# Four gate tiles of a decoder's last embedding as seven block products

## The chip, the cores and the metric

The kernel is one launch on one core of a Trainium2 chip. The core has TensorE (PE in the profile; PEld is its weight load), VectorE (DVE), ScalarE (ACT), GpSimd (POOL) and SyncE (SP, which issues the DMAs here). The metric is device time in microseconds (us): the median of several executions. A profiled execution gives one trace, whose span runs from the first to the last instruction.

## The reference

One inference step of a decoder with two layers, in float32, for 512 prompt rows and 32 sample rows, 1024 wide. Each layer ends with a gated embedding; the last one is the last thing that is computed:

```python
for i in range(DEPTH):
    h = h + 0.5 * swiglu(rmsnorm(h, ffn1_norm[i]), ffn1_w1[i], ffn1_w3[i], ffn1_w2[i])
    ...                                   # gMLP in layer 0, attention in layer 1
    h = h + 0.5 * swiglu(rmsnorm(h, ffn2_norm[i]), ffn2_w1[i], ffn2_w3[i], ffn2_w2[i])
    gate = jax.nn.sigmoid(rmsnorm(h, ple_norm[i]) @ ple_w_gate[i])     # 1024 x 1024
    h = h + gate * (pe[i] @ ple_w_proj[i])                             # 256 x 1024
```

## The kernel before

**Tiling.** The residual stream h is held transposed: 8 tiles of 128 features by 544 columns (512 prompt and 32 sample rows; T = 544, HT = 272), two tiles to a buffer. A float32 product is made of three: each operand is split into a rounded high part and the rest, and hi x hi, hi x lo and lo x hi are added in PSUM. Each is done in two halves of 272 columns, so a product over 1024 features takes 8 x 3 x 2 = 48 matmuls per output tile, and one over 256 features 12 (`mm`, L273: hi x hi at L286, hi x lo at L290, lo x hi at L292).

**Weights** come as a stream of units. `_load` (L206) issues a unit's DMA from SyncE; `_sum` (L219, VectorE at L228) adds or subtracts two raw blocks where a unit is a sum; `_split` (L231) rounds it on ScalarE (L242) and takes the rest on VectorE (L243), for a unit of 1024 columns in one instruction each. `prepare` (L247) does so some units ahead of the unit that TensorE takes, as the three numbers in `self.ahead` say: splits, sums, loads.

**Norm.** The normalised input is never formed. `prep` (L338) multiplies h with the gain and splits it, as soon as a tile of h is final; the root mean square enters at the end, as a factor on each column. `tile_rstd` (L395) slips four matmuls with ones (L408) into the first tile's product, and the reciprocal root is made by ScalarE (L386, with a load of its function table) and VectorE (L389 to L393).

**Seven block products.** The feed-forward layers compute 2 x 2 blocks of an output (two features' blocks by two column halves) with seven block products instead of eight, in the Winograd form. `seven` (L193) describes the weight units ("1", "2", "4" are raw blocks, "5", "6", "7", "3" are sums), `forms` (L347) makes the operands on the other side for two tiles of h at a time (two L352 on ScalarE; L356, L358, L359 on VectorE; two splits, L330 and L331), and the order of the products is `SEVEN = "1562734"`. One block product has 4 x 3 x 2 = 24 matmuls. Some results accumulate in one PSUM buffer: "6" goes on top of "1" once that has been copied out, and so on; the copies and additions are L547 to L561 there.

**The last embedding** is `ple` (L745) with layer 1. For c = 0 to 6 it computes a gate tile over 8 feature tiles (48 matmuls), multiplies it with the norm's factor (L766, VectorE) and takes the sigmoid (L767, ScalarE). From c = 2 on, the product of the embedding input with its projection for tile c - 2 follows (12 matmuls), is multiplied with the gate (L777), added to h (L778) and written out (L1474). Behind c = 6 come the products of tiles 5 and 6, and `ple_last` (L728) does tile 7 in column halves, so that the end of the first half overlaps the second: 48 and 12 matmuls at L723, VectorE at L736, L741 and L742, two writes at L743.

**Order.** Each engine executes its instructions strictly in the order in which they are queued. In the feed-forward layers that order is written by hand. In the embedding a scheduler of the compiler sets it, from its own times; the program then holds it fixed. Buffers come from pools: 45 large ones (big), 8 of one tile (tmp), 3 of PSUM in two banks (ps), 2 of one bank (pb); an instruction that needs a buffer waits until its last reader is through.

Of the kernel before, what the change touches and what calls it, by code (L numbers as in the profile page):

```python
# [138 lines left out]
class Builder:  # L139
# [207 lines left out]
    def forms(self, h, gcol, n, xs):  # L347
# [3 lines left out]
        for a in range(2):  # L351
# [12 lines left out]
                "5": half(f13, 0), "7": half(f13, 1), "6": half(f24, 0), "4": half(f24, 1)}  # L364
    def ssq(self, acc, h, cols=slice(0, T), first=False):
# [362 lines left out]
    def ple_last(self, h, gates, rstd, xs, wp, pp, y):  # L728

        nc, tt = self.nc, self.nc.vector.tensor_tensor  # L730
        c = NC_ - 1
        a = self.tmp()
        outs = [self.pb(), self.pb()]
        self.cols_mm(outs, self.blocks(self.unit()), xs)
        for (u, v), out in zip(COLS, outs):
# [4 lines left out]
        for (u, v), out in zip(COLS, outs):  # L740
            tt(halves(a[:, u:v]), unwoven(out[:, :v - u]), halves(a[:, u:v]), ALU.mult)  # L741
            tt(h[c][:, u:v], h[c][:, u:v], a[:, u:v], ALU.add)  # L742
            nc.sync.dma_start(out=y[c][:, u:v], in_=h[c][:, u:v])  # L743

    def ple(self, h, box, layer, on_chunk):  # L745
        nc = self.nc
        xs = self.pairs(box)
        pp = []
        for c in range(2):
            raw = self.tmp()  # L750
            nc.sync.dma_start(out=raw, in_=self.i["pe"][layer, c])
            pair = self.big(F32R)
            self.split_pair(pair, raw)
            pp.append((pair[:, 0, :], pair[:, 1, :]))
        rstd, gates, wp = None, [], []
        last = layer == 1
        for c in range(NC_ + 2):
# [15 lines left out]
            for n in (range(c - 2, c + 1) if last and c == NC_ - 2 else [c - 2] if c >= 2 else ()):  # L773
# [597 lines left out]
    def build(self):  # L1371
# [7 lines left out]
        def ple_units(n):  # L1379
            for c in range(NC_):  # L1380
# [93 lines left out]
        self.ple(h, box, 1, lambda c: nc.sync.dma_start(out=o["y"][c], in_=h[c]))  # L1474
# [123 lines left out]
```

## Time and profile before

| | us |
|---|---|
| median of 3 runs | 1932.85 |
| lowest and highest of them | 1932.0, 1933.58 |
| the profiled execution | 1931.65 |
| its span | 1929.9 |
| TensorE busy in it | 1905.2 |
| VectorE, ScalarE, GpSimd busy | 1478.6, 949.0, 143.4 |

A group of instructions reads: line, engine, operation, output<-input, partitions x elements and type, number | busy us in total, mean ns of one | idle time of the engine just before them, and what ended most of it. A row of the time line reads: start, us from the first start to the last end, engine, line, operation, number, and in brackets how long the engine had been idle and what released it. A row of a table by stage gives the stage, its length, busy us of each engine with the number of its instructions, the granted share of TensorE's clock, and the DMA engines' share and rate. Line numbers are those of the kernel before.

### The profile page before, as it was taken

How to read it: one execution, taken by the hardware profiler on the slowest of the kernel's cores; microseconds unless marked ns; L12 is line 12 of the kernel's file. 1: busy time of each engine (PE TensorE's matmuls, PEld its weight loads, DVE VectorE, ACT ScalarE, POOL GpSimd, SP SyncE). 2: the span in 40 equal slices, each digit the busy share in tenths (PEclk: the TensorE clock that was granted, in tenths of full speed). 3: DMA queues.
4: the chain of work that ended last, by engine and by line, in shares of the span. 5: the costliest groups of instructions: out<-in, count | busy, mean ns of one | idle time of the engine just before them, and what ended most of it. 6: DMA issues, size and time to landing. Idle time of an engine off the chain costs nothing.

```text
span 1929.9 us, 38975 instructions
## 1 busy us (share of the span) xinstructions
PE 1905.2 (99%) x16508; PEld 1869.9 (97%) x16508; DVE 1478.6 (77%) x1863; ACT 949.0 (49%) x1428; POOL 143.4 (7%) x190
## 2 busy tenths in 40 slices
PE   9999999999999999999999999999999999999999
PEld 8999999999999999999999999999977899999999
DVE  7878888556788888866578888887476888788874
ACT  7545444424555344454466444444374754444561
POOL 0000000400100000023000000002131300000020
PEclk9999999999999999999999999999999999999999
DMA  5233234312223232531484332323769332323431
GB/s 196 78 120 110 89 120 157 97 48 88 88 99 119 79 111 89 162 112 39 150 306 141 121 110 99 121 83 126 229 211 328 101 110 78 121 94 105 133 109 47
DMA packets 95743, 237.61 MB, mean 123 GB/s; under 512 B 11874, under 2 KB 29570, under 8 KB 95570
## 3 DMA queue, kind: packets, MB, share of 16 engines
q1 hardware_dynamic: 95426, 235.08, 36.6%
q8 instruction: 130, 2.13, 0.4%
q14 instruction: 43, 0.35, 0.1%
q10 hardware_dynamic: 144, 0.04, 0.0%
HBM read 218.65 MB, written 16.44 MB: 122 GB/s over the span
## 4 chain that ended last, share of the span: by engine, by line
PE 88%; DVE 6%; ACT 3%; issue 2%; DMA 1%; SPq 1%; POOL 0%; DVEq 0%; ACTq 0%; POOLq 0%
PE ps L539 31%; PE ps L286 15%; PE ps L292 15%; PE ps L290 15%; PE pb L539 5%; DVE big L243 2%; ACT big L242 1%; DVE big L228 1%; PE ps L892 1%; PE ps L893 1%; PE ps L894 1%; DVE big L331 1%; DVE big L497 0%; DMA tmp<-rows 0%; PE ps L1286 0%
## 5 line engine op out<-in xcount | busy, mean ns | idle before, releaser
L539 PE MATMUL ps<-big,big 128*128 128x272 f32 x5616 | 674.1, 279 | 5.9 <-DVE big L556 3.5
L539 PEld LDWEIGHTS ps<-big,big 128*128 128x128 f32 x5616 | 660.8, 189 | 7.0 <-issue 4.0
L243 DVE TENSOR_TENSOR big<-big,big 128x1024 fp32r<-128x1024 f32 (+2 forms) x537 | 587.1, 1096 | 91.0 <-ACT big L242 89.3
L242 ACT CAST big<-big 128x1024 fp32r<-128x1024 f32 (+2 forms) x537 | 484.2, 928 | 270.2 <-DVE big L228 267.7
L286 PE MATMUL ps<-big,big 128*128 128x272 f32 x2668 | 530.2, 280 | 2.9 <-ACT big L242 2.5
L292 PE MATMUL ps<-big,big 128*128 128x272 f32 x2668 | 528.3, 279 | 2.5 <-DVE big L243 2.3
L290 PE MATMUL ps<-big,big 128*128 128x272 f32 x2668 | 527.3, 279 | 0.3 <-DVE big L343 0.3
L286 PEld LDWEIGHTS ps<-big,big 128*128 128x128 f32 x2668 | 407.1, 189 | 7.8 <-ACT big L242 4.4
L292 PEld LDWEIGHTS ps<-big,big 128*128 128x128 f32 x2668 | 406.9, 189 | 4.5 <-DVE big L243 4.1
L290 PEld LDWEIGHTS ps<-big,big 128*128 128x128 f32 x2668 | 406.9, 189 | 0.7 <-DVE big L343 0.7
L371 POOL TENSOR_TENSOR st<-st,tmp 128x544 f32<-128x544 f32 (+1 forms) x63 | 87.4, 1387 | 1477.0 <-ACT tmp L369 1476.7
L228 DVE TENSOR_TENSOR big<-big,big 128x1024 f32<-128x1024 f32 x156 | 190.1, 1219 | 0.0
L578 DVE SCALAR_TENSOR_TENSOR big<-ps,big 128x544 f32<-128x544 f32 x160 | 115.3, 721 | 75.8 <-PE ps L292 75.8
L500 ACT ACTIVATE big<-big 128x544 f32<-128x544 f32 x88 | 57.9, 659 | 145.8 <-DVE big L497 144.6
L497 DVE TENSOR_TENSOR big<-big,st 128x1088 f32<-128x1088 f32 x88 | 113.6, 1293 | 3.9 <-ACT big L561 2.0
L547 ACT COPY tmp<-ps 128x544 f32<-128x544 f32 x117 | 71.5, 611 | 89.7 <-PE ps L539 89.7
L539 PE MATMUL pb<-big,big 128*128 128x272 f32 x936 | 114.8, 279 | 0.0
L539 PEld LDWEIGHTS pb<-big,big 128*128 128x128 f32 x936 | 111.3, 189 | 0.0
L342 ACT ACTIVATE big<-big,gains 128x544 fp32r<-128x544 f32 (+1 forms) x80 | 55.5, 702 | 91.3 <-DVE big L578 55.2
L331 DVE TENSOR_TENSOR big<-big,big 128x544 fp32r<-128x544 f32 (+1 forms) x112 | 79.2, 713 | 21.7 <-ACT big L330 21.5
L343 DVE SCALAR_TENSOR_TENSOR big<-big,gains,big 128x544 fp32r<-128x544 f32 (+1 forms) x80 | 64.6, 816 | 24.2 <-ACT big L342 24.2
L330 ACT CAST big<-big 128x544 fp32r<-128x544 f32 (+1 forms) x112 | 71.2, 643 | 18.9 <-DVE big L503 14.9
(218 smaller groups left out, 1388.5 us busy)
## 6 DMA issues: line engine op xcount, KB each, us to landing
big<-in_w SPq DMA_DIRECT2D x156, 512.0 KB
big<-in_w2a SPq DMA_DIRECT2D x64, 512.0 KB
big<-in_w2b SPq DMA_DIRECT2D x32, 384.0 KB
big<-in_w13p SPq DMA_DIRECT2D x16, 512.0 KB
big<-in_win SPq DMA_DIRECT2D x16, 512.0 KB
big<-in_wg SPq DMA_DIRECT2D x16, 512.0 KB
big<-in_ck SPq DMA_DIRECT2D x16, 512.0 KB
big<-in_cv SPq DMA_DIRECT2D x16, 512.0 KB
```

Of the source, the lines that this page charges most:

```text
L228: self.nc.vector.tensor_tensor(t, a, b, ALU.add if op == "+" else ALU.subtract)
L242: self.nc.scalar.copy(hi, src)
L243: self.nc.vector.tensor_tensor(lo, src, hi.bitcast(F32), ALU.subtract)
L286: i = nc.tensor.matmul(o, wh, xh[:, b], start=s, stop=False)
L290: nc.tensor.matmul(o, wh, xl[:, b], start=False, stop=False)
L292: nc.tensor.matmul(o, wl, xh[:, b], start=False, stop=e)
L331: self.nc.vector.tensor_tensor(pair[:, 1, cols], src, pair[:, 0, cols].bitcast(F32), ALU.subtract)
L371: nc.gpsimd.tensor_tensor(acc[:, cols], acc[:, cols], sq, ALU.add)
L497: tt(g, g, rstd.unsqueeze(1).broadcast_to([P, 2, T]), ALU.mult)
L539: nc.tensor.matmul(turns(dst[w]), a[:, c], woven(b), start=k in "152" and kp == 0 and n == 0, stop=kp == NKP - 1 and n == 2, skip_group_ch ...
L547: nc.scalar.copy(t["r" + k], t["C" if k == "5" else "A"])
L578: nc.vector.scalar_tensor_tensor(halves(h[c]), whole(out), 0.5, halves(h[c]), ALU.mult, ALU.add)
```

## The change

In the last embedding, the gate tiles 0 to 3 are computed as before, and all four embedding products of these tiles are put behind them. The gate tiles 4 to 7 are computed as one 2 x 2 problem by seven block products: columns 512 to 1023 of the gate's weights, re-arranged on the host into four blocks (`wg7`), against the forms of all eight tiles of h. In each of the first four gate tiles' steps, `forms` is called for two tiles of h. `strassen` repeats the evictions of the feed-forward layer, and `done` applies the norm's factor and the sigmoid to two gate tiles at once (1088 columns). Then the products of tiles 4, 6 and 5 follow, and that of tile 7 in column halves. The first embedding (layer 0) only loses its test for the last layer.

```diff
+    def strassen(self, xf, done):
+        nc, tt, t = self.nc, self.nc.vector.tensor_tensor, {}
+        u4 = lambda t: t.rearrange("p w (b a) -> p w a b", a=2)
+        h4 = lambda t: t.rearrange("p w (a b) -> p w a b", a=2)
+        def step(k):
+            hi, lo = self.unit()
+            self.advance()
+            if k == "2":
+                t["B"] = [self.pb()[:, :HT] for _ in range(2)]
+            elif k in "15":
+                t["A" if k == "1" else "C"] = self.ps()[:, :, :HT]
+            out = t["A" if k in "1674" else "C" if k in "53" else "B"]
+            for kp in range(NKP):
+                xh, xl = xf[kp][k]
+                for n, (a, b) in enumerate(((hi, xh), (hi, xl), (lo, xh))):
+                    for w in range(2):
+                        c = slice(512 * w + P * kp, 512 * w + P * kp + P)
+                        nc.tensor.matmul(turns(out[w] if k == "2" else out[:, w]), a[:, c], woven(b),
+                                         ...
+            if k in "156":
+                t["r" + k] = self.tmp().rearrange("p (w b) -> p w b", w=2)
+                nc.scalar.copy(t["r" + k], out)
+            elif k == "2":
+                t["g"] = self.big(), self.big()
+                for w in range(2):
+                    tt(halves(t["g"][0][:, w, :HT]), unwoven(out[w]), unwoven(t["r1"][:, w]), ALU.add)
+            elif k == "7":
+                tt(h4(t["g"][1][:, :, HT:]), u4(out), u4(t["r5"]), ALU.add)
+            elif k == "3":
+                tt(h4(t["g"][0][:, :, HT:]), u4(out), u4(t["r6"]), ALU.add)
+                done(0, t["g"][0])
+            else:
+                nc.scalar.copy(h4(t["g"][1][:, :, :HT]), u4(out))
+                done(1, t["g"][1])
+        return step
...
-    def ple_last(self, h, gates, rstd, xs, wp, pp, y):
+    def ple_last(self, h, box, on_chunk):
+        nc, tt, y = self.nc, self.nc.vector.tensor_tensor, self.o["y"]
+        xs, xf, a, wp, rstd = self.pairs(box), [], {}, [], None
+        pp = self.ple_input(1)
+        self.ahead = (2, 3, 6)
+        for c in range(4):
+            if rstd is None:
+                p, rstd = self.tile_rstd(xs, box["acc"])
+            else:
+                p = self.tile_mm(xs)
+            def gate(c=c, p=p):
+                a[c] = self.tmp()
+                tt(halves(a[c]), whole(p), halves(rstd), ALU.mult)
+                nc.scalar.activation(a[c], a[c], AF.Sigmoid)
+            self.evac(gate)
+            xf.append(self.forms(h, G_PLE + 8, c, xs))
+            if c < 2:
+                wp += self.blocks(self.unit())
+        def product(n):
+            p = self.ps()
+            self.mm(p, wp[2 * n:2 * n + 2], pp, True, True)
+            tt(halves(a[n]), whole(p), halves(a[n]), ALU.mult)
+            tt(h[n], h[n], a[n], ALU.add)
+            on_chunk(n)
+        def done(k, g):
+            tt(g, g, rstd.unsqueeze(1).broadcast_to([P, 2, T]), ALU.mult)
+            nc.scalar.activation(g, g, AF.Sigmoid)
+            for w in range(2):
+                a[4 + 2 * w + k] = g[:, w]
+        for n in range(4):
+            product(n)
+        step = self.strassen(xf, done)
+        for k in SEVEN:
+            step(k)
+        for n in (4, 6, 5):
+            product(n)
...
         ple_units(1)
+        d = self.seven([i["wg7"][x] for x in range(4)])
+        self.pieces.extend(d[k] for k in SEVEN)
...
-        self.ple(h, box, 1, lambda c: nc.sync.dma_start(out=o["y"][c], in_=h[c]))
+        self.ple_last(h, box, lambda c: nc.sync.dma_start(out=o["y"][c], in_=h[c]))
...
+    a["wg7"] = _pairs(ple_w_gate[1][:, D // 2:])
```

Up to the first gate tile every engine's instructions stand as before. In the rows below, a name's number is that of its buffer's allocation. The changed kernel's lines are shifted: L442, L425 and L782 are L403, L386 and L767 of before (the cast of the norm's sum, the reciprocal root, the sigmoid), L428 to L432 are L389 to L393, L781, L791, L792 are L766, L777, L778, and L811 and L812 are L741 and L742; L389 to L400 are the copies and additions in `strassen`, L796 and L797 the factor and the sigmoid in `done`.

The first place is ScalarE's queue from the cast of the norm's sum to the gate's first sigmoid. Before:

```order
L403 CAST tmp_23025<-st_22691 128x544
L242 CAST big_23045<-big_22806 128x1024
L242 CAST big_23049<-big_22856 128x1024
L242 CAST big_23112<-big_22906 128x1024
L242 CAST big_23118<-big_22956 128x1024
L386 ACT_TABLE_LOAD
L386 ACTIVATE st_23035<-pb_23029,eps 128x272
L386 ACTIVATE st_23035<-pb_23030,eps 128x272
L242 CAST big_23192<-big_23116 128x1024
L242 CAST big_23266<-big_23122 128x1024
L242 CAST big_23338<-big_23196 128x1024
L767 ACT_TABLE_LOAD
```

The same place now; big_22806 is the second unit of projection weights, big_22856 and big_22906 are the weights of gate tiles 2 and 3:

```order
L442 CAST tmp_23025<-st_22691 128x544
L352 ACTIVATE big_23045<-big_92,gains 128x544 x2
L330 CAST big_23050<-tmp_23048 128x544
L330 CAST big_23051<-tmp_23049 128x544
L242 CAST big_23059<-big_22806 128x1024
L425 ACT_TABLE_LOAD
L425 ACTIVATE st_23035<-pb_23029,eps 128x272
L425 ACTIVATE st_23035<-pb_23030,eps 128x272
L242 CAST big_23067<-big_22856 128x1024
L352 ACTIVATE big_23130<-big_93,gains 128x544 x2
L782 ACT_TABLE_LOAD
L782 ACTIVATE tmp_23075<-tmp_23075 128x544
```

The cast of tile 2's weights has moved from the third row to behind the first forms, the table load and the reciprocal root. That of tile 3's weights, the fourth row before, comes only behind the second sigmoid and two more L330, after the last row shown.

The second place is VectorE's queue around the weights of block products "5" and "6" (big_23154 and big_23226 are their sums), which had no counterpart before:

```order
L791 TENSOR_TENSOR tmp_23205<-ps_23326,tmp_23205 128x544
L243 TENSOR_TENSOR big_23223<-big_23154,big_23222 128x1024
L228 TENSOR_TENSOR big_23226<-big_23154,big_22956 128x1024
L792 TENSOR_TENSOR big_93<-big_93,tmp_23205 128x544
L791 TENSOR_TENSOR tmp_23277<-ps_23342,tmp_23277 128x544
L356 TENSOR_TENSOR tmp_23283<-big_23280 128x544
L792 TENSOR_TENSOR big_93<-big_93,tmp_23277 128x544
L358 TENSOR_TENSOR tmp_23284<-big_23280,tmp_23283 128x272
L331 TENSOR_TENSOR big_23285<-tmp_23283,big_23285 128x544
L359 TENSOR_TENSOR tmp_23284<-big_23280,tmp_23284 128x272
L331 TENSOR_TENSOR big_23286<-tmp_23284,big_23286 128x544
L243 TENSOR_TENSOR big_23359<-big_23226,big_23358 128x1024
```

Between the sum for "6" (L228) and its split (the last row) stand the ends of products 2 and 3 and the last set of forms, whose second half "6" reads.

The third place is VectorE's end. Before, behind tile 6:

```order
L777 TENSOR_TENSOR tmp_23459<-ps_23494,tmp_23459 128x544
L778 TENSOR_TENSOR big_95<-big_95,tmp_23459 128x544
L736 TENSOR_TENSOR tmp_23510<-pb_23511,st_23035 128x272
L736 TENSOR_TENSOR tmp_23510<-pb_23512,st_23035 128x272
L741 TENSOR_TENSOR tmp_23510<-ps_23565,tmp_23510 128x272
L742 TENSOR_TENSOR big_95<-big_95,tmp_23510 128x272
L741 TENSOR_TENSOR tmp_23510<-ps_23566,tmp_23510 128x272
L742 TENSOR_TENSOR big_95<-big_95,tmp_23510 128x272
```

Now, from the eviction of block product "3":

```order
L397 TENSOR_TENSOR big_23484<-ps_23395,tmp_23452 128x2x272
L796 TENSOR_TENSOR big_23484<-big_23484,st_23035 128x1088
L791 TENSOR_TENSOR big_23484<-ps_23571,big_23484 128x544
L796 TENSOR_TENSOR big_23485<-big_23485,st_23035 128x1088
L792 TENSOR_TENSOR big_94<-big_94,big_23484 128x544
L791 TENSOR_TENSOR big_23484<-ps_23587,big_23484 128x544
L791 TENSOR_TENSOR big_23485<-ps_23603,big_23485 128x544
L811 TENSOR_TENSOR big_23485<-ps_23619,big_23485 128x272
L792 TENSOR_TENSOR big_95<-big_95,big_23484 128x544
L792 TENSOR_TENSOR big_94<-big_94,big_23485 128x544
L811 TENSOR_TENSOR big_23485<-ps_23620,big_23485 128x272
L812 TENSOR_TENSOR big_95<-big_95,big_23485 128x272 x2
```

Where one tile's multiplications and additions were left behind the last gate, now those of four tiles are.

More of the change, by code (lines that the diff above doesn't have):

```diff
@@ L364, in forms @@
                 "5": half(f13, 0), "7": half(f13, 1), "6": half(f24, 0), "4": half(f24, 1)}
+    def strassen(self, xf, done):
[16 more added lines that the diff above has]
+                        nc.tensor.matmul(turns(out[w] if k == "2" else out[:, w]), a[:, c], woven(b),
+                                         start=k in "152" and kp == 0 and n == 0, stop=kp == NKP - 1 and n == 2,
+                                         skip_group_check=True)
+            if k in "156":
[14 more added lines that the diff above has]
+        return step
     def ssq(self, acc, h, cols=slice(0, T), first=False):
@@ L740, in ple_last, with ple_input @@
         for (u, v), out in zip(COLS, outs):
-            tt(halves(a[:, u:v]), unwoven(out[:, :v - u]), halves(a[:, u:v]), ALU.mult)
-            tt(h[c][:, u:v], h[c][:, u:v], a[:, u:v], ALU.add)
+            tt(halves(a[c][:, u:v]), unwoven(out[:, :v - u]), halves(a[c][:, u:v]), ALU.mult)
+            tt(h[c][:, u:v], h[c][:, u:v], a[c][:, u:v], ALU.add)
             nc.sync.dma_start(out=y[c][:, u:v], in_=h[c][:, u:v])
+    def ple_input(self, layer):
+        pp = []
+        for c in range(2):
+            raw = self.tmp()
+            self.nc.sync.dma_start(out=raw, in_=self.i["pe"][layer, c])
+            pair = self.big(F32R)
+            self.split_pair(pair, raw)
+            pp.append((pair[:, 0, :], pair[:, 1, :]))
+        return pp
     def ple(self, h, box, layer, on_chunk):
@@ L747, in ple @@
         xs = self.pairs(box)
[L748 to L754, printed above, removed]
+        pp = self.ple_input(layer)
         rstd, gates, wp = None, [], []
-        last = layer == 1
         for c in range(NC_ + 2):
@@ L772, in ple @@
                 wp += [(hi[:, P * k:P * k + P], lo[:, P * k:P * k + P]) for k in range(8)]
-            for n in (range(c - 2, c + 1) if last and c == NC_ - 2 else [c - 2] if c >= 2 else ()):
+            for n in [c - 2] if c >= 2 else ():
                 p2 = self.ps()
@@ L1379, in ple_units @@
         def ple_units(n):
-            for c in range(NC_):
+            for c in range(4 if n else NC_):
                 self.add_plain(i["wg"][n, c])
@@ L1487, in _blocks, with _pairs @@
     return w.reshape(k // 256, 2, P, m // 256, 2, P).transpose(3, 4, 1, 2, 0, 5).reshape(m // 256, 4, P, k // 256, P)
+def _pairs(w):
+    h = w.shape[1] // 2
+    return np.stack([_blocks(w[:, :h]), _blocks(w[:, h:])], 3).reshape(4, P, 1024)
 def _constants():
```

10 lines of the change are left out of this document (removed).

## The prediction

> **What bounds the kernel now.** I read the page's busy shares first, then the last 150 us cut into stages, then the end of the time line.
>
> ```profile
> span 1929.9 us, 38975 instructions
> PE 1905.2 (99%) x16508; PEld 1869.9 (97%) x16508; DVE 1478.6 (77%) x1863; ACT 949.0 (49%) x1428; POOL 143.4 (7%) x190
> ```
>
> ```profile
> core 0: us, PE busy (x) PEld busy (x) DVE busy (x) ACT busy (x) POOL busy (x), PEclk, DMA share, GB/s
> 1779.00:1870.00 91.00, 91.00 (x788) 91.00 (x788) 72.58 (x84) 45.12 (x63) 9.65 (x6) 1.00 0.42 128
> 1870.00:1885.00 15.00, 15.00 (x132) 15.00 (x131) 13.50 (x16) 11.79 (x15) 1.34 (x1) 1.00 0.01 2
> 1885.00:1890.00 5.00, 5.00 (x45) 5.00 (x45) 4.23 (x6) 3.15 (x4) 0.00 (x0) 1.00 0.02 3
> 1890.00:1926.00 36.00, 35.98 (x311) 35.78 (x309) 12.92 (x21) 3.48 (x6) 0.00 (x0) 1.00 0.15 55
> 1926.00:1928.00 2.00, 0.00 (x0) 0.00 (x0) 1.11 (x3) 0.00 (x0) 0.00 (x0) 1.00 0.20 70
> 1928.00:1929.90 1.90, 0.00 (x0) 0.00 (x0) 0.00 (x0) 0.00 (x0) 0.00 (x0) 0.51 0.20 73
> ```
>
> TensorE has no gap from 1779 to its last matmul. The last embedding (from 1869.76) has two halves: until 1890 VectorE works 17.73 of 20 us and ScalarE 14.94, nearly full; after 1890 they work 12.92 and 3.48 of 36, and wait for TensorE. The first half has no slack; the second has 23 us on VectorE.
>
> ```profile
> 1918.87 5.72 PE L723 MATMUL pb<-big,big 128*128 128x272 f32 x48
> 1924.43 1.55 PE L723 MATMUL ps<-big,big 128*128 128x272 f32 x12
> 1925.39 0.44 DVE L741 TENSOR_TENSOR tmp<-ps,tmp 128x272 f32<-128x272 f32 x1 [0.32 <-PE ps L723]
> 1926.34 1.16 SPq L743 DMA_DIRECT2D out_y<-big  x2
> 1926.70 0.44 DVE L742 TENSOR_TENSOR big<-big,tmp 128x272 f32<-128x272 f32 x1
> ```
>
> 48 matmuls in 5.72 us, the last 0.28 long, are 0.1157 us apart. TensorE ends at 1925.98, VectorE at 1927.14, and the span 2.76 us later, with the last writes.
>
> **The change part by part.** Removed: the gate of tiles 4 to 7 goes from 192 to 168 matmuls, 24 x 0.1157 = **-2.78 us**. Nothing else leaves TensorE.
>
> Added, on the engines that prepare: 4 sets of block operands (per set 2 L352 and 2 L330 on ScalarE; L356, L358, L359 and 2 L331 on VectorE), 4 weight sums (L228), 3 more weight casts and splits (10 in place of 7). Prices:
>
> ```profile
> L243 DVE TENSOR_TENSOR big<-big,big 128x1024 fp32r<-128x1024 f32 x377 | 464.7, 1236 | 77.3 <-ACT big L242 76.9
> L242 ACT CAST big<-big 128x1024 fp32r<-128x1024 f32 x377 | 388.6, 1043 | 270.2 <-DVE big L228 267.7 <-PE ps L539 1.6 <-DMA big<-in_w13p 0.7
> L228 DVE TENSOR_TENSOR big<-big,big 128x1024 f32<-128x1024 f32 x156 | 190.1, 1219 | 0.0
> L497 DVE TENSOR_TENSOR big<-big,st 128x1088 f32<-128x1088 f32 x88 | 113.6, 1293 | 3.9 <-ACT big L561 2.0
> L547 ACT COPY tmp<-ps 128x544 f32<-128x544 f32 x117 | 71.5, 611 | 89.7 <-PE ps L539 89.7
> L352 ACT ACTIVATE big<-big,gains 128x544 f32<-128x544 f32 x32 | 22.1, 740 | 0.0
> L356 DVE TENSOR_TENSOR tmp<-big 128x544 f32<-128x544 f32 x16 | 11.9, 744 | 5.3 <-ACT big L352 5.1
> L778 DVE TENSOR_TENSOR big<-big,tmp 128x544 f32<-128x544 f32 x15 | 10.9, 724 | 0.5
> L358 DVE TENSOR_TENSOR tmp<-big,tmp 128x272 f32<-128x272 f32 x16 | 7.6, 476 | 0.5
> ```
>
> VectorE: 4 x (0.74 + 0.48 + 0.48 + 2 x 0.72) + 4 x 1.22 + 3 x 1.24 = 21 us on top of 31 in the stage. There is room for that only after 1890, but each engine takes its queue in order, and the queue rows above show operands and the sigmoid's table load ahead of weight casts that TensorE needs next. So I follow the queues, with these rows of the same place:
>
> ```profile
> 1859.33 7.47 SPq L209 DMA_DIRECT2D big<-in_wg  x3
> 1869.76 0.40 PE L286 MATMUL ps<-big,big 128*128 128x272 f32 x2
> 1871.92 1.18 ACT L330 CAST big<-tmp 128x544 fp32r<-128x544 f32 x2
> 1873.53 0.65 ACT L403 CAST tmp<-st 128x544 fp32r<-128x544 f32 x1 [0.43 <-POOL st L371]
> 1874.08 3.88 ACT L242 CAST big<-big 128x1024 fp32r<-128x1024 f32 x4
> 1877.98 1.28 ACT L386 ACT_TABLE_LOAD   x1
> 1879.28 0.87 ACT L386 ACTIVATE st<-pb,eps 128x272 f32<-128x272 f32 x2
> 1881.01 0.79 DVE L392 SCALAR_TENSOR_TENSOR tmp<-pb,tmp 128x272 f32<-128x272 f32 x2
> 1875.28 4.62 DVE L243 TENSOR_TENSOR big<-big,big 128x1024 fp32r<-128x1024 f32 x4
> 1884.62 1.35 DVE L766 TENSOR_TENSOR tmp<-ps,st 128x544 f32<-128x544 f32 x2
> 1885.41 1.28 ACT L767 ACT_TABLE_LOAD   x1 [2.44 <-DVE tmp L766]
> 1886.71 1.87 ACT L767 ACTIVATE tmp<-tmp 128x544 f32<-128x544 f32 x3
> ```
>
> Back to back, an operation starts some 0.1 us before the one ahead has ended: L243 1.13 apart ((4.62 - 1.22) / 3), L242 0.95, 544-wide VectorE operations 0.63, L330 0.54, the sigmoid 0.6, and so L352 0.65; L331 is taken as L778. The loads stand where they stood and land 20 us before use: nothing. What a wait costs shows in the feed-forward stage:
>
> ```profile
> 1531.06 0.50 PE L286 MATMUL ps<-big,big 128*128 128x272 f32 x2 [0.64 <-ACT big L242]
> ...
> 1532.32 0.50 PE L292 MATMUL ps<-big,big 128*128 128x272 f32 x2 [0.53 <-DVE big L243]
> 1562.66 0.73 PE L539 MATMUL ps<-big,big 128*128 128x272 f32 x4 [1.31 <-ACT tmp L547]
> 1560.00:1565.00 5.00, 3.69 (x32) 3.49 (x31) 3.89 (x4) 2.85 (x4) 0.00 (x0) 1.00 0.23 93
> ```
>
> A tile whose weights come late waits twice: for the cast, and after four matmuls for the split (L243 1.22 long, the four cover 0.46). Two matmuls after a wait take 0.50 instead of 0.40: 0.10 more each time.
>
> (a) Gate tile 2. TensorE is through tiles 0 and 1 and the four matmuls of the norm at 1869.76 + 100 x 0.1157 = 1881.33. ScalarE is free at 1874.08; two L352 until 1875.47; L356 until 1876.2, L358 and L359 until 1877.25; the second L330 lets go at 1877.8; L242 of the projection weights until 1878.85; table load 1880.15; two L425 1880.9; L242 for tile 2 1881.95. Waits 0.65 and 0.7, restarts 0.2: **+1.55**. Tile 2 ends at 1888.4.
>
> (b) Gate tile 3. Behind the split of (a) stand two L431, L432 and L781 (0.79 + 0.72 + 0.72), until 1885.4, as before. Then the table load to 1886.7, two sigmoids 1887.9, two L330 1889.0, L242 1890.05: **+1.75**. Its split is covered by products 0 and 1 (24 matmuls, 2.78 us).
>
> (c) Piece 6. TensorE has 156 matmuls until there: 1888.4 + 1.75 + 18.05 = 1908.2. VectorE, from 1890.4: two L243 and an L228 (3.4), six 544-wide (3.8), L358 and L359 (0.8), 1898.4; it waits for tile 3, 1898.7; three 544-wide, 1900.6; L243 and L228, 1902.9; four 544-wide, 1905.4; L358, L331, L359, 1906.95; L330, L242 on ScalarE, 1908.6; L243, 1909.85. Waits 0.4 and 0.7, restarts 0.2: **+1.3**. Pieces 6, 2 and 7 end at 1912.3, 1915.1 and 1917.9.
>
> (d) Piece 3. Copying piece 6 out (L389) holds ScalarE until 1913.0; L242 and L243 of piece 7, then the sum, 1916.45; L242 1917.5, L243 1918.75; TensorE had its four matmuls done at 1918.35: **+0.5**. Piece 3 ends at 1921.2, piece 4 at 1924.0: the 424 matmuls until there alone would end at 1869.76 + 49.06 = 1918.8, and 5.1 are waits.
>
> (e) The end. Behind piece 3: L397 to 1922.2, L796 (as L497) to 1923.5, the sigmoid of 1088 columns. No row has that: between 0.66 (544 columns) and 1.31 (two of them); I take 1.1, since a cast grows from 0.65 to 1.04 from 544 to 1024. ScalarE 1924.6; L400 copies piece 4, 1925.2; L796 1926.5; then VectorE has nine operations left, five of 544 (3.15) and four of 272 (1.5): 1931.2. TensorE has 30 matmuls behind piece 4, until 1927.5; the last six wait for a PSUM buffer that VectorE frees near 1928, and end at 1928.8, ahead of their place in that queue. VectorE ended at 1927.14 before: **+4.1**. In the terms above: -2.78, + 5.1, + 0.4 for the buffer, and 1.3 that the queue behind TensorE's end is longer (2.4 for 1.16), in all +4.0; the walk rounds up. Where before two half writes were left, now two whole ones (272 KB) stand shortly ahead of them: 0 to 0.6 us, I take 0.1, as each now starts 0.6 behind the other.
>
> Sum: +4.2 us on the profiled execution's 1931.65 us: 1935.9. The median of the runs is 1.2 above it: **1937.1 us**. 0.2% of 1932.85 is 3.87 us, about what a measurement of this kernel can tell from no change, so the forecast lies just on the slower side of it.
>
> **Rivals.** *All waits covered.* The feed-forward stage runs the same seven pieces at 91.00 of 91.00 us with VectorE at 72.58: they can be fed. It would take L242 of tile 2 before 1881.33 and of tile 3 before 1888.4. Then only -2.78 + 1.3 is left: 1931.4, not slower. Against it: there, operands are made a stage ahead; here they start when the stage does. Even with no longer end it is -2.78, which is less than 3.87. [...]
>
> *First half only.* (a) and (b) come, as they hang on few operations, but VectorE makes up time after 1890, where it was 36% busy, and (c) and (d) vanish: 4.2 - 1.8 = +2.4, 1935.2. For it: the slack. Against it: in the walk VectorE has no gap over 0.4 us from 1890.4 to 1907, so it has nothing to catch up with.
>
> *The clock falls.* It was still 1.00 in the 2 us after TensorE's last matmul and 0.51 after them; a wait of 1.31 at 1562 left it at 1.00. Wait (b), 1.65, lies between. If it fell, and took the same 2 us to return, matmuls at half speed would lose 1.0; if it stayed for a tile, 5.55: 1938 to 1942.6. [...]
>
> *It doesn't do what it says.* The rows show 168 matmuls for 192 and the same loads, so no.
>
> **How the numbers follow.** Forecast 0.60. Clock or a longer queue 0.05, slower too. First half only 0.25 and all covered 0.07, both within 0.2%. Still better, 0.03, the only way to faster, as the whole saving is under 3.87. So slower 0.65, same 0.32, faster 0.03. The forecast alone: (e) -0.45 to +0.2, writes to +0.5, the runs' own spread 1932.0 to 1933.58, say 1936.0 to 1938.6. The range goes down to just under the second rival and up to a short fall of the clock: 1935.0 to 1939.4.
>
> **What would show it.** TensorE's first gap on L242 at 1881.3 and one of some 1.7 us at 1888.4, both in the old window where it had none; a gap on L242 or L243 near piece 6 and near piece 3; VectorE's nine last operations running without a gap behind L796; TensorE's last matmul near 1928.8; clock 1.00. Wrong if no wait longer than 1 us stands before 1895, or if TensorE's last matmul comes before 1926.

## The result, and the profile after

The median of 20 runs of the changed kernel is 1936.78 us (1934.99 to 1940.75), that of 20 runs of the kernel before beside them 1932.41 us (1930.83 to 1933.92): ratio 1.0024, 95% interval 1.0018 to 1.0030. The change makes the kernel 4.4 us slower, with 24 matmuls fewer. The profiled execution took 1936.29 us. Two runs of the experiments below, at 2804 and 4038 us, were slow ones and are left out of the ratios (the two medians count them).

The first view is the page of the changed kernel, its span and busy shares:

```profile
span 1934.4 us, 38971 instructions
PE 1905.6 (99%) x16484; PEld 1869.1 (97%) x16484; DVE 1498.3 (77%) x1891; ACT 963.4 (50%) x1448; POOL 142.7 (7%) x190
```

VectorE has 19.7 us more than before (1478.6) and ScalarE 14.4 (949.0), on a core whose shares of the span change by one percent at most. The table by stage of the changed kernel shows where it counts (stretch, its length, busy us of TensorE, its weight loads, VectorE, ScalarE and GpSimd with their instructions, the granted share of TensorE's clock, DMA share and rate):

```profile
1779.00:1870.00 91.00, 91.00 (x788) 91.00 (x787) 72.73 (x84) 45.15 (x63) 9.67 (x6) 1.00 0.40 125
1870.00:1892.00 22.00, 19.50 (x164) 18.89 (x163) 17.93 (x26) 17.18 (x25) 1.34 (x1) 1.00 0.04 17
1892.00:1907.00 15.00, 15.00 (x132) 15.00 (x131) 14.72 (x22) 6.28 (x10) 0.00 (x0) 1.00 0.17 63
1907.00:1920.00 13.00, 11.81 (x98) 11.20 (x97) 9.00 (x11) 6.60 (x8) 0.00 (x0) 1.00 0.04 14
1920.00:1929.30 9.30, 9.19 (x76) 8.64 (x74) 7.88 (x11) 2.72 (x3) 0.00 (x0) 1.00 0.08 32
1929.30:1931.60 2.30, 0.00 (x0) 0.00 (x0) 2.21 (x5) 0.00 (x0) 0.00 (x0) 0.90 0.40 155
```

Up to 1870 it is the kernel before. Then TensorE stands still for 2.5 us before 1892 and for 1.2 between 1907 and 1920, where before it did not stand still at all; and VectorE works 2.2 us longer than TensorE. The clock is 1.00 up to TensorE's last matmul. TensorE's time line names each wait (in brackets how long the engine had been idle, and what released it; rows between are left out):

```profile
1881.32 0.40 PE L292 MATMUL ps<-big,big 128*128 128x272 f32 x2
1882.23 0.50 PE L286 MATMUL ps<-big,big 128*128 128x272 f32 x2 [0.52 <-ACT big L242]
1882.57 0.40 PE L290 MATMUL ps<-big,big 128*128 128x272 f32 x2
1883.49 0.50 PE L292 MATMUL ps<-big,big 128*128 128x272 f32 x2 [0.53 <-DVE big L243]
...
1888.46 0.39 PE L292 MATMUL ps<-big,big 128*128 128x272 f32 x2
1890.31 0.50 PE L286 MATMUL ps<-big,big 128*128 128x272 f32 x2 [1.45 <-ACT big L242]
...
1907.79 0.86 PE L384 MATMUL ps<-big,big 128*128 128x272 f32 x6
1908.89 0.73 PE L384 MATMUL ps<-big,big 128*128 128x272 f32 x4 [0.25 <-ACT big L242]
1910.15 2.58 PE L384 MATMUL ps<-big,big 128*128 128x272 f32 x20 [0.53 <-DVE big L243]
...
1915.36 3.41 PE L384 MATMUL ps<-big,big 128*128 128x272 f32 x28
1919.17 5.58 PE L384 MATMUL ps<-big,big 128*128 128x272 f32 x44 [0.41 <-DVE big L243]
```

Gate tile 2 waits for its cast and again for its split, gate tile 3 for its cast, piece 6 (block product "6") for both, piece 3 for its split. The bracket counts from the modelled end of the matmul ahead; what is lost is more: two matmuls are 0.23 apart, so 1882.23 comes 0.68 after the 1881.55 at which it could have started. Ahead of these waits, ScalarE's queue:

```profile
1879.09 1.28 ACT L425 ACT_TABLE_LOAD   x1
1880.38 0.87 ACT L425 ACTIVATE st<-pb,eps 128x272 f32<-128x272 f32 x2
1881.14 1.04 ACT L242 CAST big<-big 128x1024 fp32r<-128x1024 f32 x1
...
1885.73 1.28 ACT L782 ACT_TABLE_LOAD   x1 [2.27 <-DVE tmp L781]
1887.03 1.20 ACT L782 ACTIVATE tmp<-tmp 128x544 f32<-128x544 f32 x2
1888.13 1.18 ACT L330 CAST big<-tmp 128x544 fp32r<-128x544 f32 x2
1889.22 1.99 ACT L242 CAST big<-big 128x1024 fp32r<-128x1024 f32 x2
```

The cast of tile 2's weights (1881.14) stands behind forms, table load and reciprocal root; that of tile 3's (1889.22) behind a second table load, two sigmoids and two more casts, though ScalarE is idle for 2.27 us ahead of them. It is the order of the queue that makes TensorE wait, while the engine that it waits for is idle.

The end, from the time line of the changed kernel:

```profile
1922.56 1.29 DVE L796 TENSOR_TENSOR big<-big,st 128x1088 f32<-128x1088 f32 x1
1923.88 1.11 ACT L797 ACTIVATE big<-big 128x1088 f32<-128x1088 f32 x1 [5.07 <-DVE big L796]
1927.37 1.86 PE L762 MATMUL ps<-big,big 128*128 128x272 f32 x12
1928.27 0.76 PEld L762 LDWEIGHTS ps<-big,big 128*128 128x128 f32 x6 [0.25 <-DVE big L791]
1930.73 0.78 DVE L812 TENSOR_TENSOR big<-big,big 128x272 f32<-128x272 f32 x2
```

TensorE ends at 1929.23, VectorE at 1931.51, the span 2.9 behind it.

### The profile page after: what moved, and what is told of

Read it like the earlier page. It is cut to its first block, busy times and chain, and to the rows that moved or that the text cites. A ratio compares the mean times of both kernels' runs of the same rounds, so it can differ in the third digit from the quotient of the medians.

```text
span 1934.4 us, 38971 instructions
## 1 busy us (share of the span) xinstructions
PE 1905.6 (99%) x16484; PEld 1869.1 (97%) x16484; DVE 1498.3 (77%) x1891; ACT 963.4 (50%) x1448; POOL 142.7 (7%) x190
## 3 DMA queue, kind: packets, MB, share of 16 engines
q8 instruction: 130, 2.13, 0.4%
## 4 chain that ended last, share of the span: by engine, by line
PE 86%; DVE 7%; ACT 4%; issue 2%; DMA 1%; SPq 0%; POOL 0%; POOLq 0%; DVEq 0%; ACTq 0%
PE ps L578 31%; PE ps L286 14%; PE ps L292 14%; PE ps L290 14%; PE pb L578 5%; DVE big L243 2%; ACT big L242 2%; DVE big L228 1%; PE ps L962 1%; PE ps L963 1%; PE ps L964 1%; DVE big L331 1%; DVE big L536 0%; PE ps L1356 0%; DMA big<-in_x 0%
## 5 line engine op out<-in xcount | busy, mean ns | idle before, releaser
L578 PE MATMUL ps<-big,big 128*128 128x272 f32 x5616 | 674.1, 279 | 5.6 <-DVE big L595 3.5
L578 PEld LDWEIGHTS ps<-big,big 128*128 128x128 f32 x5616 | 660.8, 189 | 6.7 <-issue 4.0
L243 DVE TENSOR_TENSOR big<-big,big 128x1024 fp32r<-128x1024 f32 (+2 forms) x540 | 591.0, 1097 | 94.5 <-ACT big L242 92.9
L242 ACT CAST big<-big 128x1024 fp32r<-128x1024 f32 (+2 forms) x540 | 487.6, 929 | 272.1 <-DVE big L228 269.8
L286 PE MATMUL ps<-big,big 128*128 128x272 f32 x2620 | 521.4, 280 | 4.8 <-ACT big L242 4.2
L292 PE MATMUL ps<-big,big 128*128 128x272 f32 x2620 | 519.3, 280 | 2.9 <-DVE big L243 2.7
L290 PE MATMUL ps<-big,big 128*128 128x272 f32 x2620 | 518.6, 279 | 0.3 <-DVE big L343 0.3
L286 PEld LDWEIGHTS ps<-big,big 128*128 128x128 f32 x2620 | 400.4, 189 | 10.1 <-ACT big L242 6.6
L292 PEld LDWEIGHTS ps<-big,big 128*128 128x128 f32 x2620 | 400.2, 189 | 5.0 <-DVE big L243 4.5
L290 PEld LDWEIGHTS ps<-big,big 128*128 128x128 f32 x2620 | 400.1, 189 | 0.5 <-DVE big L343 0.5
L228 DVE TENSOR_TENSOR big<-big,big 128x1024 f32<-128x1024 f32 x160 | 195.0, 1219 | 0.0
L578 PE MATMUL pb<-big,big 128*128 128x272 f32 x936 | 114.8, 279 | 0.0
L578 PEld LDWEIGHTS pb<-big,big 128*128 128x128 f32 x936 | 111.3, 189 | 0.0
L343 DVE SCALAR_TENSOR_TENSOR big<-big,gains,big 128x544 fp32r<-128x544 f32 (+1 forms) x80 | 64.6, 817 | 25.3 <-ACT big L342 25.3
L330 ACT CAST big<-big 128x544 fp32r<-128x544 f32 (+1 forms) x112 | 71.1, 643 | 18.9 <-DVE big L542 15.0
```

What stands on the lines that cost most here:

```text
L228: self.nc.vector.tensor_tensor(t, a, b, ALU.add if op == "+" else ALU.subtract)
L242: self.nc.scalar.copy(hi, src)
L243: self.nc.vector.tensor_tensor(lo, src, hi.bitcast(F32), ALU.subtract)
L286: i = nc.tensor.matmul(o, wh, xh[:, b], start=s, stop=False)
L290: nc.tensor.matmul(o, wh, xl[:, b], start=False, stop=False)
L292: nc.tensor.matmul(o, wl, xh[:, b], start=False, stop=e)
```

## The experiments

The traced executions reach the last feed-forward stage's first update of h between 1846.1 and 1849.5 us, by what happens long before. So, beside the medians, each kernel's own stretch is compared: from VectorE's first update of h in the last feed-forward stage (the group L578 of the kernel before, its eighth operation from the end) to VectorE's end. These are its ends before and after:

```profile
1846.33 0.72 DVE L578 SCALAR_TENSOR_TENSOR big<-ps,big 128x544 f32<-128x544 f32 x1 [1.74 <-PE ps L292]
```
```profile
1846.53 0.72 DVE L617 SCALAR_TENSOR_TENSOR big<-ps,big 128x544 f32<-128x544 f32 x1 [1.72 <-PE ps L292]
```

Before it is 1927.14 - 1846.33 = 80.81 us, after 1931.51 - 1846.53 = 84.98. All kernels, in us, each with its difference from the kernel before and the one that was expected of it; the medians are of 5 to 31 runs, each with the kernel before on the same chip. A stretch is that of one traced execution; the medians' differences lie within 0.9 us of it, but for *forms early* (9.3 for 7.66):

| kernel | stretch | difference | expected | median, before beside it | ratio (95%) |
|---|---|---|---|---|---|
| the change | 84.98 | +4.17 | +4.1 | 1936.78, 1932.41 | 1.0024 (1.0018 to 1.0030) |
| without forms | 79.02 | -1.79 | -1.8 | 1930.80, 1932.21 | 0.9996 (0.9987 to 1.0005) |
| without sums | 83.00 | +2.19 | +2.2 | 1935.25, 1932.21 | 1.0016 (1.0007 to 1.0024) |
| order alone | 81.32 | +0.51 | +0.5 | 1932.54, 1932.21 | 1.0002 (0.9993 to 1.0011) |
| forms unused | 84.64 | +3.83 | +3.8 | 1936.51, 1932.21 | 1.0027 (1.0016 to 1.0038) |
| hand order | 83.57 | +2.76 | -1.3 | 1934.49, 1932.52 | 1.0008 (0.9999 to 1.0017) |
| hand order, other end | 82.56 | +1.75 | -2.3 | 1934.54, 1932.52 | 1.0007 (0.9998 to 1.0016) |
| split further ahead | 84.94 | +4.13 | +3.4 | 1937.04, 1932.52 | 1.0020 (1.0011 to 1.0029) |
| forms early | 88.47 | +7.66 | +5.6 | 1941.78, 1932.52 | 1.0045 (1.0031 to 1.0059) |
| second hand order | 78.95 | -1.86 | -2.1 | 1930.63, 1932.17 | 0.9991 (0.9982 to 0.9999) |
| norm's additions on VectorE | 80.96 | +0.15 | level | 1933.10, 1932.17 | 1.0004 (0.9995 to 1.0012) |

### What the waits come from: one part left out, or one part alone

**Without forms.** The products read halves of the normalised tiles where the change has forms.

```diff
-            xf.append(self.forms(h, G_PLE + 8, c, xs))
+            xf.append({k: tuple(x[:, (HT if k in "734" else 0):][:, :HT]
+                                for x in xs[2 * c + (k in "2364")]) for k in SEVEN})
```

> Seven block products as in the change, but without the forms: the products read raw halves of the normalised tiles in place of the sums and differences, so the last four gate tiles come out as other numbers; the sums of weights, the order of the products and the end stay. My account (the waits are the forms' doing): gate tiles 2 and 3 and pieces 6 and 3 no longer wait; TensorE's last matmul near 1923.2 us of the trace and VectorE's end near 1925.3, so about 1.8 us faster than the kernel before (the 2.78 saved, less 1.0 for the longer end). Rival (the products themselves, their evictions and the longer end are the price): the time stays near the changed kernel's, 3 to 4 us slower than before.

The waits at gate tiles 2 and 3 and at pieces 6 and 3 are gone, and the stretch is 1.79 shorter than before. By the medians it is 1.4 faster, by the ratio not to be told from before. The block products themselves cost what their matmuls cost, 2.78 less; 0.2 is lost in one short wait of TensorE (at 1887.5), and 0.8 in the longer end (VectorE 1.92 behind TensorE, before 1.16), for which 1.0 was expected.

**Without sums.** The four sums of weights are left out.

```diff
         d = self.seven([i["wg7"][x] for x in range(4)])
+        for k, x in (("5", 0), ("6", 1), ("7", 2), ("3", 3)):
+            d[k].update(sum=None, src=(len(self.aps) - 4 + x, 0))
```

> Seven block products with their forms, but the four sums of weights are left out (each of these pieces takes a raw block, so the last four gate tiles come out as other numbers). My account: the waits of gate tiles 2 and 3 stay as they are (0.5 + 0.5 and 1.45 us), since no sum stands ahead of them; those at pieces 6 and 3 go, since four VectorE operations of 1.22 us fewer stand in the queue. TensorE's last matmul about 2.1 earlier than in the changed kernel, VectorE's end near 1929.3; about 2.2 us slower than before. Rival (the first half's waits come from too much work in all): they shrink too, and the time is within 1 us of before. Rival (pieces 6 and 3 wait for the forms alone): the time is that of the changed kernel.

All of TensorE's waits in the embedding of this kernel:

```profile
1883.52 0.50 PE L286 MATMUL ps<-big,big 128*128 128x272 f32 x2 [0.52 <-ACT big L242]
...
1884.78 0.50 PE L292 MATMUL ps<-big,big 128*128 128x272 f32 x2 [0.53 <-DVE big L243]
...
1891.60 0.50 PE L286 MATMUL ps<-big,big 128*128 128x272 f32 x2 [1.45 <-ACT big L242]
...
1927.57 0.96 PE L762 MATMUL ps<-big,big 128*128 128x272 f32 x6 [0.26 <-DVE big L791]
```

The waits of gate tiles 2 and 3 are the same to a hundredth; those at pieces 6 and 3 are gone, and 1.98 us with them. So the first half's waits owe nothing to the amount of later work, and the second half's need the sums as well as the forms.

**The order alone,** with plain gate tiles, and **the forms unused,** which adds the forms to that (the call of `forms` goes in the first and stays in the second; in both `strassen` gives way to four gate tiles):

```diff
-        step = self.strassen(xf, done)
-        for k in SEVEN:
-            step(k)
+        for c in range(4, NC_):
+            p = self.tile_mm(xs)
+            a[c] = self.tmp()
+            tt(halves(a[c]), whole(p), halves(rstd), ALU.mult)
+            nc.scalar.activation(a[c], a[c], AF.Sigmoid)
```

> Only the order of the change: gate tiles 4 to 7 as plain products of 48 matmuls, with the embedding products of tiles 0 to 3 in front of them and those of 4, 6, 5 and 7 behind them; no forms and no sums. My account: no wait on TensorE, its last matmul at 1926 as before, VectorE's end 0.5 later since more additions are left behind the last gate; 0.5 us slower than before, that is, not to be told from it. Rival (the order is what costs): 1.5 to 4 us slower.

> The order of the change with plain gate tiles, and the forms computed where the change computes them, but not used. My account: gate tiles 2 and 3 wait as in the changed kernel (about 0.6, 0.6 and 1.5 us with their restarts 0.3), pieces that follow do not; TensorE's last matmul near 1929.1, VectorE's end near 1930.9; about 3.8 us slower than before. Rival (the block products' own evictions hold the engines): no wait, and the time of the kernel with the order alone.

The order costs 0.51. The forms, computed for nothing, cost another 3.32, with the waits of the change (0.53, 0.53 and 1.46 in the brackets) and no others. That is what tiles 2 and 3 lose in the change: 1.58 + 1.72, below.

### Whether another order does better

**Split further ahead.** One number tuple changed:

```diff
-        self.ahead = (2, 3, 6)
+        self.ahead = (3, 4, 7)
```

> The changed kernel with one number changed: weights are split three units ahead in place of two, summed four and loaded seven ahead. My account (the order of the queues decides): the casts of gate tiles 2 and 3 stand ahead of the forms, so these waits go, but the forms and the evictions come later, and TensorE waits for the next weights, and for a PSUM buffer, some 2.2 and 0.7 us around 1897 to 1901; pieces 6 and 3 still wait some 0.5 each; about 3.4 us slower than before. Rival (the waits at tiles 2 and 3 are a matter of how far ahead the weights are): some 2.5 us better than the changed kernel, 1.5 slower than before.

The waits at tiles 2 and 3 went, and one wait took their place, behind the gate tiles and the first two embedding products (L791 reads their PSUM buffers and so frees them); after it TensorE was slow for a while. Time line, and then the table by stage:

```profile
1895.18 0.40 PE L292 MATMUL ps<-big,big 128*128 128x272 f32 x2
1898.23 0.50 PE L286 MATMUL ps<-big,big 128*128 128x272 f32 x2 [2.65 <-DVE tmp L791]
...
1898.85 0.66 PE L292 MATMUL ps<-big,big 128*128 128x272 f32 x2
...
1902.02 0.46 PE L286 MATMUL ps<-big,big 128*128 128x272 f32 x2
```
```profile
1898.20:1898.80 0.60, 0.57 (x4) 0.57 (x5) 0.60 (x2) 0.00 (x0) 0.00 (x0) 0.94 0.00 0
1898.80:1902.10 3.30, 3.30 (x17) 3.30 (x16) 3.30 (x7) 1.02 (x2) 0.00 (x0) 0.50 0.35 135
```

Pairs of matmuls come 0.45 apart in place of 0.23 for 3.4 us: the granted clock had halved 0.5 us after TensorE went on, and some 1.6 us went with it ((3.17 us from 1898.85 to 1902.02) - 14 x 0.1157). Of the waits that were expected, the first came 0.6 longer (2.8 from where TensorE could have gone on), and the second (0.7) and that at piece 6 (0.5) did not come; with the clock's 1.6 that makes 1.0, where the forecast was missed by 0.7. Both accounts were too cheap, mine less: splitting further ahead only moved the wait, and its price grew as the clock fell behind it.

**Forms early.** Tiles 0 to 3's forms by the kernel's own means, in the last feed-forward stage:

```diff
-        on, nxt = self.next_norm(h, G_PLE + 8)
+        on, nxt = self.next_norm(h, G_PLE + 8, early={1: 0, 3: 1})
```

> The changed kernel with the forms of tiles 0 to 3 made in the last feed-forward stage, each set in one piece as soon as its second tile is final, as the kernel does elsewhere. My account: VectorE waits for ScalarE within each set while the next tile's update stands behind it, so the feed-forward stage itself gets a wait of about 1.4 us, and the gate tiles wait at another place (2.8 and 0.7 at about 1886, 1.7 at about 1894): 5.6 us slower than before, worse than the change. Rival (early operands are all that is missing): the waits at tiles 2 and 3 go, 1 to 1.5 us slower than before.

Worse than the change, as expected, and by more: the feed-forward stage waited 1.93, a gate tile waited 2.54 at 1887.9, and after each of the two the clock fell (table by stage, clock 0.62 and 0.65), which cost some 1.6 each time; the wait of 1.7 expected at about 1894 did not come:

```profile
1867.70:1871.00 3.30, 3.29 (x18) 3.30 (x19) 3.30 (x4) 3.07 (x5) 1.56 (x1) 0.62 0.59 207
1887.90:1891.50 3.60, 3.06 (x14) 2.86 (x15) 3.53 (x6) 1.33 (x3) 0.00 (x0) 0.65 0.00 0
```

**A hand-written order, and another end.** `ple_last` is written out by hand for TensorE, ScalarE and VectorE, the weights come in the order gate 0 to 3, projection, blocks, and two sets of forms are spread over the last feed-forward tiles (`on0` is the norm's work for output tile c, `g(0, 4)` four steps of the first set, with three subtractions and two casts). The second kernel also applies factor and sigmoid to quarters (`scale`, columns s of two tiles):

```diff
+        with self.tc.manual_schedule(engines={eng.PE, eng.Activation, eng.DVE, eng.Pool}):
+            self.ple_hand(h, box, on_chunk)
...
+            on0(c)
+            if c == 4:
+                g(0, 4)
...
+        def scale(g, s, out=None):
+            tt(h4(g[:, :, s]), h4(g[:, :, s]) if out is None else u4(out), part(s), ALU.mult)
```

> Everything of the change, with another order: ScalarE's, VectorE's and TensorE's queues are written by hand. The forms of the first two pairs of tiles are made, a few operations per output tile, in the idle time of the last feed-forward stage; the weights of the gate tiles stand first in the stream, ahead of the projection's; sums and splits stand ahead of the evictions that can wait. The common end of two gate tiles stays as in the change. My account (the waits come from the order, not from too much work): no wait on TensorE, its last matmul 2.8 earlier than before, and VectorE's end 1.3 earlier than before; about 1.3 us faster than before. Rival (the added 21 us of VectorE and the added ScalarE work don't fit, the waits move elsewhere): within 1 us of the changed kernel, or worse, as the last feed-forward stage is held up too.

> The hand-written order, and another end: the norm's factor and the sigmoid are applied to a quarter of the block problem as soon as it is final (544 columns each in place of 1088, piece 4 scaled straight out of PSUM), and the embedding products of tiles 4 and 6 stand around piece 4, so that only those of 5 and 7 are behind it. My account: TensorE as in the hand order, VectorE's end another 1.0 earlier, 2.3 us before that of the kernel before: about 2.3 us faster than before, the version that beats both. Rival (the end is bound by VectorE's sum of work, not by how it is cut): as the hand order alone, 1.3 faster.

Both were missed by 4.1 us, and by the same 4.1. The other end is worth 2.76 - 1.75 = 1.01 in these two executions, as expected, though their medians (1934.49 and 1934.54) do not show it. The 4.1 are waits of TensorE: 3.2 in four waits at the start of the embedding (0.81, 0.62, 0.45 and 0.26 in the second kernel's brackets), and 0.9 ahead of the first block product, for a PSUM buffer that the eviction of gate tile 3 frees. The first came since the feed-forward stage was late: its last four updates of h on VectorE took from 1860.60 to 1877.14, 16.5 us, where before they took 12.5. VectorE's and GpSimd's time lines of the second kernel, where the forms were put:

```profile
1862.37 0.78 DVE L343 SCALAR_TENSOR_TENSOR big<-big,gains,big 128x544 fp32r<-128x544 f32 x1
1863.07 1.86 DVE L375 TENSOR_TENSOR tmp<-big 128x544 f32<-128x544 f32 x1
...
1868.74 0.78 DVE L343 SCALAR_TENSOR_TENSOR big<-big,gains,big 128x544 fp32r<-128x544 f32 x1
1869.43 1.88 DVE L386 TENSOR_TENSOR big<-tmp,big 128x544 fp32r<-128x544 f32 x1
```
```profile
1862.86 1.49 POOL L441 TENSOR_TENSOR st<-st,tmp 128x544 f32<-128x544 f32 x1 [2.18 <-ACT tmp L439]
1868.90 1.83 POOL L441 TENSOR_TENSOR st<-st,tmp 128x544 f32<-128x544 f32 x1 [4.55 <-ACT tmp L439]
```

A subtraction that takes 0.72 elsewhere took 1.86 and 1.88. GpSimd's addition ended at 1864.35 and 1870.73, VectorE's operations 0.58 behind it each time: as if they had begun only when it was through. The norm's addition is there in every tile, in the kernel before from 2.1 to 2.3 us after VectorE's update on, and so lies over the very time in which VectorE had been counted as idle.

**The norm's additions on VectorE** test that, in the kernel with the other end:

```diff
-            self.ssq(box["acc"], h[c], cols, first=c == 0)
+            if gcol == G_PLE + 8 and c:
+                sq = self.tmp()[:, cols]
+                self.nc.scalar.activation(sq, h[c][:, cols], AF.Square)
+                self.nc.vector.tensor_tensor(box["acc"][:, cols], box["acc"][:, cols], sq, ALU.add)
+            else:
+                self.ssq(box["acc"], h[c], cols, first=c == 0)
```

> The hand order with the other end (forms of the first two pairs in the feed-forward stage), with one thing changed: the seven additions of this norm's squares run on VectorE in place of GpSimd. My account (a VectorE addition from SBUF and a GpSimd addition exclude each other): the first subtraction of each early set of forms lasts 0.72 in place of 1.86 us, and although VectorE has 7 x 0.64 more to do, VectorE's end comes 1.5 us earlier than with the GpSimd additions, level with the kernel before. Rival (the long operations come from something else, a DMA or the ScalarE writes beside them): they stay at 1.86, and the time gets 2 to 4 us longer than in the hand order with the other end.

```profile
1863.43 0.72 DVE L375 TENSOR_TENSOR tmp<-big 128x544 f32<-128x544 f32 x1
...
1869.29 0.72 DVE L386 TENSOR_TENSOR big<-tmp,big 128x544 fp32r<-128x544 f32 x1
```

The same two operations, 0.72 each, and the stretch 1.60 shorter (82.56 to 80.96) although VectorE has seven additions more to do. The rival is out: the length came from GpSimd's addition. It is not the whole of the 4.1: the 0.9 ahead of the first block product stay, and so does some of the wait at the start, with VectorE's own additions now in that stage.

**The second hand order** takes the consequence. Only ScalarE's multiplications are moved ahead; the forms are made in the embedding behind the last GpSimd addition, and piece 3 is put ahead of piece 7, so that the copy of piece 6 that piece 7 waits for is covered (`g(0, 1)` is ScalarE's part of the first set):

```diff
+            on0(c)
+            if c == 4:
+                g(0, 1)
+            if c == 5:
+                g(1, 1)
+            if c == 6:
+                g(2, 1)
...
+        self.add_plain(i["wp"][1, 0])
+        self.pieces.append(d["1"])
+        self.add_plain(i["wp"][1, 1])
+        self.pieces.extend(d[k] for k in "256374")
```

> A second hand-written order, after what the first showed: VectorE's additions and subtractions from SBUF lasted 1.86 in place of 0.72 us wherever a GpSimd addition of the norm ran beside them, so nothing of the forms but ScalarE's multiplication is moved into the last feed-forward stage. All forms are made in the embedding, behind the last GpSimd addition, sorted by when TensorE needs them; block products in the order 1, 2, 5, 6, 3, 7, 4; additions to h and writes as late as they may be; the end in quarters. My account (the changed kernel's waits come from the order of the queues): feed-forward stage as before, no wait over 0.1 us on TensorE in the embedding, last matmul 2.6 and VectorE's end 2.1 before those of the kernel before: 2.1 us faster, 6 us better than the change. Rival (the added 21 us on VectorE do not fit whatever the order): waits of 2 us or more in all, no faster than before.

The table by stage of this kernel, the rows that answer to those of before:

```profile
1780.00:1870.40 90.40, 90.40 (x783) 90.40 (x782) 72.00 (x83) 48.96 (x69) 9.66 (x6) 1.00 0.40 129
1870.40:1890.00 19.60, 19.60 (x171) 19.60 (x171) 16.81 (x27) 15.65 (x23) 1.34 (x1) 1.00 0.01 2
1890.00:1910.00 20.00, 20.00 (x175) 20.00 (x174) 19.52 (x26) 8.37 (x11) 0.00 (x0) 1.00 0.04 15
1910.00:1924.20 14.20, 14.13 (x119) 13.62 (x117) 13.05 (x19) 5.02 (x7) 0.00 (x0) 1.00 0.25 92
```

TensorE is all but full to the end again, VectorE works 19.52 of 20 us in the middle, and the stretch is 1.86 shorter than before. The median is 1930.63, 1.5 below the kernel before beside it (the interval, 0.9982 to 0.9999, ends just short of no change) and 6.2 below the change. So this is the version that beats both, the one narrowly. What is missing of the expected 2.1 lies in TensorE's last 14 us: it loses 0.3 at 1913.1, waiting for a split (L833, through at 1913.01), and 0.2 at 1917.0, right behind an addition that reads a PSUM buffer (L1019, through at 1916.81).

## Why the prediction was right, step by step

Forecast were +4.2 us on the profiled execution and a median of 1937.1. The profiled execution took 4.64 more (1936.29 for 1931.65), of which 0.2 lies ahead of the stage, 0.1 outside the span, and 4.3 in the stage (4.17 to VectorE's end, 0.13 in the last writes). The median is 1936.78, 4.37 above the kernel before beside it. That it was met to 0.3 is in part luck: the kernel before came out 0.44 lower in its 20 runs than in the three that the forecast stood on, and among the terms, in us, (d) was too small and (e) too large:

| step | forecast | measured | how |
|---|---|---|---|
| matmuls | -2.78 | -2.78 | 168 for 192 |
| (a) gate tile 2 | +1.55 | +1.58 | 0.68 late for the cast, 0.69 for the split (1883.49 for 1882.80), two restarts of 0.10 |
| (b) gate tile 3 | +1.75 | +1.72 | 1890.31 for 1888.69, one restart |
| (c) piece 6 | +1.3 | +1.3 | 0.40 and 0.70, two restarts |
| (d) piece 3 | +0.5 | +0.9 | 0.57, a restart, and 0.23 more up to 1924.59 |
| (e) PSUM buffer | +0.4 | +0.3 | the last 12 matmuls in 1.86, before in 1.55 |
| (e) longer end | +1.3 | +1.1 | VectorE 2.28 behind TensorE, before 1.16 |
| (e) writes | +0.1 | +0.1 | 2.89 behind VectorE, before 2.76 |

Measured, they sum to 4.3; the forecast's sum to 4.1, which its walk rounded up to 4.2. The mechanism is that of the forecast, wait by wait. **Mis-sized was (d):** it ended the stage's waits with piece 3's split. The 44 matmuls from 1919.17 on took 5.42, where 44 x 0.1157 and a restart are 5.19. Piece 4 adds onto the buffer of piece 7, whose eviction (the addition L395) stands on VectorE behind the split of piece 4's weights and ran from 1920.87 to 1921.59, when piece 3's matmuls were all but through. The trace has the gap just there: the first matmul of piece 4 starts at 1921.73, 0.25 behind the one ahead of it and 0.14 behind the end of L395. That is read from these times; no run tries it. The sigmoid of 1088 columns, for which there was no row, was taken as 1.1 and measured 1.11.

**The rivals.** *All waits covered* and *first half only* are out by the trace: the waits at pieces 6 and 3 came, as VectorE had nothing to spare in between (14.72 of 15.00 us from 1892 to 1907). But the ground on which *all waits covered* stood was sound: the operands can be fed, by another order. The second hand order lies 1.5 us below the kernel before, as much as this rival gave (1931.4 for 1932.85), though with another end. Of the 2.78 us that TensorE has less to do, 1.86 show in its stretch, and in the change none.

*The clock falls* did not come to pass in the profiled execution: the clock was 1.00 up to TensorE's last matmul, with a wait of 1.45 by the bracket. This rival went by the length of a wait, between 1.31 and 2.0, and that alone does not decide. The trace of before has a wait of 2.14 at 546.58 that left the clock at 1.00, while after waits of 1.93, 2.54 and 2.65 in the experiments it was at a half for 3.4 us. About 1.6 us were lost each time; the price of 1.0 that the forecast gave it was too low, since the clock took 3.4 us to return there and not 2. Whether one of the longer of the 20 runs (up to 1940.75) had such a fall can't be said, as one execution has a trace.

Of what was to show it: the first gaps came at 1881.6 and 1888.7, on L242 both; the nine last operations ran without a gap behind L796; TensorE's last matmul ended at 1929.2 (forecast 1928.8, from a start 0.2 earlier).

## What to carry to other kernels

This change took 2.78 us of work from the busiest engine and added to the engines that feed it (19.7 us on VectorE, 14.4 on ScalarE). With such a change, follow their queues, instruction by instruction, from where the new work stands to the next thing that the busy engine needs, and don't add up shares. If the waits come from the order (here TensorE lost 5.8 us in one order and 0.5 in another, with nearly the same operations), write the order by hand before giving up the change. And before work is put into an engine's idle time, look at what the other engines do in just that time (here a subtraction of 0.72 us took 1.86 beside a GpSimd addition).

## What the runs showed of the hardware that was not expected

**VectorE's additions and subtractions with their operands in SBUF took longer beside a GpSimd addition.** In *hand order, other end* two such VectorE operations of 544 columns lasted 1.86 and 1.88 in place of 0.72 us, and ended 0.58 behind the GpSimd addition; with the GpSimd additions moved away they lasted 0.72 at the same place. The kernel before pays for this too: in its last feed-forward stage two L243 of 768 columns lasted 1.48 and 1.47, and 0.95 each with the additions moved away. In *hand order, other end* GpSimd's addition lasted 1.49 and 1.83 when it began 0.29 and 0.62 ahead of the end of VectorE's L343 (1862.37 + 0.78, 1868.74 + 0.78), which comes to some 1.2 from that end on, as if it had waited too. VectorE's updates out of PSUM ran beside it at their 0.72 (in the kernel before L578 from 1850.81 on, with GpSimd's addition from 1850.70 to 1852.11). How this comes about was not shown.

**TensorE's clock** fell to a half after some waits, and the length of a wait alone does not say after which: one of 2.14 us left it at 1.00, and after one of 2.13 it was at 0.50. This is one wait early in the program, in the kernel before, and then in *split further ahead*, with the row of the table by stage behind it:

```profile
546.58 5.68 PE L539 MATMUL ps<-big,big 128*128 128x272 f32 x47 [2.14 <-DVE big L556]
```
```profile
546.72 5.50 PE L578 MATMUL ps<-big,big 128*128 128x272 f32 x31 [2.13 <-DVE big L595]
547.30:550.30 3.00, 3.00 (x15) 3.00 (x15) 3.00 (x4) 1.36 (x3) 0.00 (x0) 0.50 0.00 0
```

In the kernel before the clock stayed at 1.00 from 544 to 552 us, and so it did in eight of the other kernels; in *split further ahead*, *forms early* and *hand order, other end* it fell there (clock 0.88, 0.94 and 0.89 from 544 to 548 us, 0.69, 0.63 and 0.68 from 548 to 552). Counted at half the clock, that is 3.4 us in each of the three. The falls near the end lasted as long: behind the wait of 2.65 in *split further ahead* (0.84 from 1896 to 1900, 0.73 from 1900 to 1904), and behind those of 1.93 and 2.54 in *forms early* (0.57 from 1868 to 1872; 0.62 from 1888 to 1892 and 0.95 from 1892 to 1896). They came some 0.5 us after the matmuls went on in the first, and some 0.8 and 1.0 in the other two, estimated from the clock's shares above. What decides whether a wait is followed by a fall was not shown.
